# The end of an RG-LRU mixer: gating of the last head by halves on two engines, last products by halves, weight splitting and router scaling on GpSimd

## The chip, the core and the metric

The kernel runs on one core of a Trainium2 chip. The metric is the device time of one execution in microseconds. The engines are TensorE (PE, with its weight loads as PEld), VectorE (DVE), ScalarE (ACT), GpSimd (POOL) and SyncE (SP), which issues the weight transfers. Each executes its own instructions in program order, and semaphores order them against each other.

## The reference

A latent stream of 256 tokens of width 1024 runs through two layers, with 256 context tokens as a prefix. Layer 0 has a bidirectional RG-LRU mixer, layer 1 a spatial-gating mixer, and a mixture of 64 experts stands behind each. All is float32. The part that matters here is the output of the first mixer and the router behind it:

```python
for d in range(2):                                   # both directions
    a_x, b_x = lru_coeffs(flip(ux), ...)
    b_x = b_x.at[:, 0].add(a_x[:, 0] * h_c[:, -1])   # start from the context's state
    yx = yx + flip(linear_scan(a_x, b_x))
out_x = (jax.nn.gelu(gate_x) * yx) @ w_out           # width 1280 = 5 heads x 256
...
x = x + g1 * yx
hx = rmsnorm(x, ffn_norm_g[i]) * (1.0 + sc2) + sh2
scores = jax.nn.sigmoid(jnp.dot(hx, router_w))       # top 8 of 64, by groups
```

## The kernel before

Features lie on the partitions: a head of 256 features is two feature tiles, jt = 0 and jt = 1, of 128 partitions x 256 tokens. Float32 products are made from fp32r parts: each operand x is split into hi = fp32r(x) and lo = x - hi, and `mm3` (line 311) issues hi*hi, hi*lo and lo*hi. Weights come from memory as 1 MB tiles of 128x2048 in a ring. `splitter` (line 555) makes their parts: ScalarE casts hi (wh, line 566), and VectorE or GpSimd, as `split_eng` (line 709) says, subtracts lo (wl, line 567). In this mixer a tile is split by two halves of 128x1024, and four buffers hold wh and wl, so two tiles.

The schedule is written by hand: an engine's instructions stand in the order in which the Python program issues them. The list plan0 gives the order of the steps: for each head h a step A (input projection and convolution), C (gate projection, gelu), B (recurrence gates), mixed with steps F (products of the modulation weights), then O(0) to O(3) and Q. O(i) makes the output products of two of the eight output tiles with the features of heads 0 to 3 (48 products of 128x256 each), and Q adds those of head 4 (48 products in all) for all eight. `ready(n)` makes the weight parts up to number n be split. Step O(i) first splits the tile of O(i+1), so O(0) splits the rest of O(1), O(1) the two halves of O(2), O(2) those of O(3), and O(3) those of Q.

The recurrence itself is in `B_end` (line 860), one call for each feature tile: a multiply of 128x1024, four scans of 128x256 and one add on VectorE. The calls for head 4 are issued by `release()` in O(0), behind that step's `ready`, for jt = 0, and in O(1), behind that step's `ready`, for jt = 1. Behind the second one `gated(4)` follows: multiply by the gelu gate in place (line 902), cast to zh (line 909), subtract to zl (line 910), all on VectorE and 128x512, both feature tiles at once.

Ahead of O(2) a `Tail` is made. Its constructor scales the router weights by s2 on VectorE (rws, line 597; s2 itself at line 511), and issues 16 small products on TensorE. In Q, each of four steps adds 12 products to one PSUM bank, `tail.flush()` issues the router's products for the previous two output tiles, and `tail.add` puts the finished output into the residual stream (line 608), squares it on ScalarE (line 617) and adds the squares on GpSimd (line 621). Behind the last flush the MoE starts: the norm, the routing on VectorE, and the order of the experts, which the queue of the expert weights waits for (line 376).

Of the kernel before, what the change touches and what calls it, by code (L numbers as in the profile page):

```python
# [10 lines left out]
F32 = mybir.dt.float32  # L11
# [4 lines left out]
OP = mybir.AluOpType  # L16

P = 128
D = 1024
KD = 8  # L20
T = 256
# [282 lines left out]
def _body(nc, tc, a, pp, rp, ps, ps1, dr):  # L304
    V, S, G, PE = nc.vector, nc.scalar, nc.gpsimd, nc.tensor
    st = Stream(nc)

    def mm(out, lhsT, rhs, start, stop):
        PE.matmul(out, lhsT, rhs, start=start, stop=stop, skip_group_check=True)  # L309

    def mm3(out, wh, wl, xh, xl, start, stop):

        mm(out, wh, xh, start, False)
        mm(out, wh, xl, False, False)
        mm(out, wl, xh, False, stop)
# [194 lines left out]
    def scale_of(out, sc, g):  # L510
        V.scalar_tensor_tensor(out=out, in0=sc, scalar=1.0, in1=g, op0=OP.add, op1=OP.mult)
# [43 lines left out]
    def splitter(tmp, tiles, eng, bufs=4, per=1):  # L555

        out = []

        def get(q, last=None):
            while len(out) < min(q + 3, last or 4 * len(tiles)):  # L560
                i, c = divmod(len(out), 4)
                n = 512 * per
                t = st.tile(tiles[i])[:, 512 * c:512 * c + n]
                hi = tmp.tile([P, n], F32R, name="wh", bufs=bufs)
                lo = tmp.tile([P, n], F32R, name="wl", bufs=bufs)
                S.copy(out=hi, in_=t)  # L566
                eng(i, c).tensor_tensor(out=lo, in0=t, in1=hi.bitcast(F32), op=OP.subtract)  # L567
                out.extend((hi[:, o:o + 512], lo[:, o:o + 512]) for o in range(0, n, 512))
                if c + per == 4:
                    st.free(tiles[i])  # L570
            return out[max(q, 0)]

        return get

    def cut(parts, c):
        return [x[:, c * P:c * P + P] for x in parts]

    class Tail:


        def __init__(self, tmp, l, gain, rw, name, bufs, per=2, some=6):
            self.per, self.some = per, some
            self.tmp, self.l, self.gain, self.router = tmp, l, gain, rw is not None
            self.name, self.bufs = name, bufs

            self.csh = rs_d[:, 1, 0:64]
            self.p = ps1.tile([P, 512], F32, name="s")
            self.ss = self.p[:, 192:194]
            self.rt = self.p[:, 0:128].rearrange("p (t e) -> p t e", t=2)
            self.sh = self.p[:, 128:192]  # L590
            self.first = True
            self.pend = []
            if rw is not None:
                s2 = later["s2"]
                self.rws = rws = tmp.tile([P, 8, 64], F32, name="rws", bufs=1)
                scale_of(s2, mod[:, l, 4, :], later["ffng"][:, l, :])
                V.tensor_tensor(out=rws, in0=rw, in1=s2.unsqueeze(2).to_broadcast([P, 8, 64]), op=OP.mult)
                for k in range(8):
                    self._mm(self.sh, mod[:, l, 3, k:k + 1].to_broadcast([P, P]), rw[:, k, :], k == 7)

# [39 lines left out]
    def mixer0(rx):  # L640
      with tc.tile_pool(name="m0", bufs=1) as mp, tc.tile_pool(name="m0t", bufs=2) as tp:
# [6 lines left out]
        zh = mp.tile([P, 10, T], F32R, name="zh")  # L648
        zl = mp.tile([P, 10, T], F32R, name="zl")
        ys, gs = {}, {}  # L650
        rw = mp.tile([P, 8, 64], F32, name="rw")
# [26 lines left out]
        for half in range(2):  # L678
            q = [qc[k // 4] if half else qx[:, k:k + 4] for k in (0, 4)]
# [3 lines left out]
            q = q[0]  # L683
# [19 lines left out]
        s2 = mp.tile([P, 2, 10], F32, name="s2")  # L703
# [4 lines left out]

        def split_eng(i, c):
            kind, j = plan0[users[i]]  # L710
            return G if (kind, j) == ("A", 0) or kind == "O" else V


        base = 8
        wq = splitter(tp, [2] + [base + i for i in users[1:]], split_eng, 4, 2)

        def ready(n):
# [142 lines left out]
        def B_end(h, jt, y, ta, te, ti):  # L860
            V.memset(te[:, 0, T:T + 1], 0.5)
            V.memset(te[:, 1, 2 * T - 1:2 * T], 0.5)
            V.tensor_tensor(out=ti, in0=ti, in1=te, op=OP.mult)
            for d in range(2):
                r_, s_, i_ = ta[:, d, :], te[:, d, :], ti[:, d, :]
                rv = (lambda z: z[:, ::-1]) if d else (lambda z: z)
                V.tensor_tensor_scan(rv(s_[:, T:]), rv(r_[:, T:]), rv(i_[:, T:]), 0.0, OP.mult, OP.add)
                last = T if d else 2 * T - 1
                dst = s_[:, :T] if d else y[:, jt, :]
                V.tensor_tensor_scan(rv(dst), rv(r_[:, :T]), rv(i_[:, :T]), s_[:, last:last + 1], OP.mult, OP.add)  # L870
                if d:
                    V.tensor_tensor(out=y[:, jt, :], in0=y[:, jt, :], in1=dst, op=OP.add)
            if jt:
                if h < 4:
                    done.append(h)
                else:
                    gated(h)()

        def Cg(i, q):
            p = bank()  # L880
# [10 lines left out]
        ob = {}  # L891

        def release():
            if held:
                if not rooted:
                    roots()
                rooted.popleft()
                B_end(*held.popleft())

        def gated(h):  # L900
            yv, gv = ys.pop(h), gs.pop(h)
            V.tensor_tensor(out=yv, in0=yv, in1=gv, op=OP.mult)

            def parts():
                hi, lo = (z[:, 2 * h:2 * h + 2, :] for z in (zh, zl))
                if h < 3:
                    S.copy(out=hi, in_=yv)
                else:
                    V.tensor_copy(out=hi, in_=yv)
                V.tensor_tensor(out=lo, in0=yv, in1=hi.bitcast(F32), op=OP.subtract)  # L910

            return parts
# [9 lines left out]
                        j == 0 and f == 0, False)  # L922

        def Q(_, q):
            wq(q + 1)
            for i in range(4):
                for j in range(2):
                    for f in range(2):
                        mm3(ob[i][:, j * T:(j + 1) * T], *cut(wq(q + 2 * f + i // 2), 2 * i % 4 + j), zh[:, 8 + f, :], zl[:, 8 + f, :],
                            False, f == 1)  # L930
                tail.flush()
                for j in range(2):
                    tail.add(2 * i + j, ob[i][:, j * T:(j + 1) * T])
# [745 lines left out]
```

## Time and profile before

| | |
|---|---|
| median of 3 runs | 1469.41 us (1467.08 to 1471.1) |
| profiled execution | 1469.6 us |
| its span, first to last instruction | 1467.7 us |
| mean granted TensorE clock | 0.980 |
| TensorE busy | 1392.4 us (95%) |
| VectorE busy | 753.6 us (51%) |
| ScalarE busy | 518.7 us (35%) |
| GpSimd busy | 331.8 us (23%) |
| moved by DMA | 514.85 MB, mean 351 GB/s |

The times of the profile are counted from the first instruction; the first mixer ends at about 248 us. A busy share is an average over stages with different limits, so the stretch of the change has to be read by itself: what each engine did there in order of time, and which wait ended last. A row of a timeline gives the start, the duration, the engine, the line, the operation, the tile written and the tiles read, and in brackets the idle time of the engine ahead of it with what ended it. The granted clock is given as a share of the upper level of 2.4 GHz.

### The profile page before, as it was taken

What the parts mean: (1) busy time and instruction counts of PE and PEld (TensorE: products, weight loads), DVE (VectorE), ACT (ScalarE), POOL (GpSimd) and SP (SyncE); (2) the same over time, 40 slices, a digit from 0 to 9 for tenths busy, and PEclk for the clock granted to TensorE, in tenths of its full rate; (3) what the DMA queues carried; (4) which work ended last, traced back from release to release, by engine and by line L of the source; (5) the groups of instructions that cost most, each with busy time, mean ns of one, the idle gap of its engine ahead of it and who ended that gap; (6) DMA issues with size and microseconds to landing.
All of it is one profiled execution on the core that took longest, in us unless ns stands there. A gap on an engine that the chain in (4) does not pass through costs nothing. (4 is left out here: it accounts for less than half of the span.)

```text
span 1467.7 us, 27203 instructions
## 1 busy us (share of the span) xinstructions
PE 1392.4 (95%) x10752; PEld 973.3 (66%) x10752; DVE 753.6 (51%) x1375; ACT 518.7 (35%) x874; POOL 331.8 (23%) x415
## 2 busy tenths in 40 slices
PE   6999997899999999999999999899999999999997
PEld 4677776656566575666657899775656666566664
DVE  6789997524343333334346786542334334343534
ACT  4777882422122222222225445432212222212222
POOL 1300044421222112312001451431212212111210
PEclk9999999899999999999999999999999999999999
DMA  9876694589989999999999744369999999999994
GB/s 376 321 276 245 245 375 186 222 351 409 412 362 405 420 420 420 420 418 421 420 418 388 289 163 173 116 251 412 394 389 372 421 421 421 420 419 420 420 420 182
DMA packets 77443, 514.85 MB, mean 351 GB/s; under 512 B 9856, under 2 KB 10240, under 8 KB 17024
## 3 DMA queue, kind: packets, MB, share of 16 engines
q1 hardware_dynamic: 74720, 508.91, 85.3%
q10 hardware_dynamic: 2592, 4.16, 0.9%
q8 instruction: 86, 1.41, 0.4%
q14 instruction: 45, 0.37, 0.1%
HBM read 511.99 MB, written 1.05 MB: 350 GB/s over the span
## 5 line engine op out<-in xcount | busy, mean ns | idle before, releaser
L309 PE MATMUL b<-wr,xg 128*32 128x512 f32 (+2 forms) x1464 | 306.5, 600 | 4.6 <-DMA wr<-in_m_gu 2.9
L567 POOL TENSOR_TENSOR wl<-wr,wh 128x512 fp32r<-128x512 f32 (+1 forms) x82 | 121.2, 1492 | 704.5 <-ACT wh L566 654.5
L309 PE MATMUL b<-wx,xg 128*32 128x512 f32 (+2 forms) x744 | 234.3, 598 | 1.7 <-SPq L1430 1.4
L566 ACT CAST wh<-wr 128x512 fp32r<-128x512 f32 (+1 forms) x230 | 147.4, 682 | 84.5 <-PE b L309 44.8
L567 DVE TENSOR_TENSOR wl<-wr,wh 128x512 fp32r<-128x512 f32 (+1 forms) x148 | 145.4, 1010 | 57.6 <-ACT wh L566 57.4
L309 PEld LDWEIGHTS b<-wr,xg 128*32 128x32 f32 (+2 forms) x1464 | 83.9, 118 | 134.9 <-issue 119.5
L1159 DVE SCALAR_TENSOR_TENSOR xT<-b,mod,xT 128x256 f32<-128x256 f32 x304 | 130.0, 478 | 60.5 <-PE b L309 54.5
L309 PE MATMUL s<-hh,wh 128*128 128x256 f32 x512 | 152.3, 297 | 1.1 <-ACT wh L566 1.1
L309 PE MATMUL s<-hh,wl 128*128 128x256 f32 x512 | 145.5, 284 | 3.7 <-DVE wl L567 1.9
L1526 DVE TENSOR_TENSOR h<-h,b 128x256 f32<-128x256 f32 x44 | 18.5, 420 | 252.4 <-ACT h L1525 252.4
L309 PE MATMUL s<-hl,wh 128*128 128x256 f32 x512 | 144.7, 283 | 0.0
L309 PE MATMUL b<-wr,ht 128*32 128x512 f32 (+2 forms) x712 | 141.9, 596 | 1.5 <-ACT ht L1535 1.5
L1549 DVE SCALAR_TENSOR_TENSOR Y<-b,gt,Y 128x512 fp32r<-128x512 f32 x88 | 65.8, 750 | 150.8 <-ACT Y L1548 150.8
L1525 ACT ACTIVATE h<-b 128x256 f32<-128x256 f32 x44 | 16.9, 384 | 351.0 <-PE b L309 351.0
L309 PEld LDWEIGHTS s<-hh,wh 128*128 128x128 f32 x512 | 98.2, 192 | 28.7 <-issue 25.3
L309 PE MATMUL b<-wx,ht 128*32 128x512 f32 (+2 forms) x392 | 109.1, 595 | 0.5 <-ACT ht L1535 0.5
L1548 ACT ACTIVATE Y<-b,gt 128x512 fp32r<-128x512 f32 x88 | 60.3, 687 | 135.8 <-PE b L309 129.5
L309 PEld LDWEIGHTS s<-hh,wl 128*128 128x128 f32 x512 | 98.1, 192 | 4.8 <-DVE wl L567 2.5
L1407 POOL TENSOR_SCALAR S<-cst,agq 128x32 fp32r<-128x32 f32 (+3 forms) x208 | 83.2, 429 | 72.2 <-PE b L309 54.5
L567 POOL TENSOR_TENSOR wl<-wx,wh 128x512 fp32r<-128x512 f32 (+1 forms) x36 | 53.6, 1506 | 199.2 <-ACT wh L566 192.6
L309 PEld LDWEIGHTS s<-hl,wh 128*128 128x128 f32 x512 | 98.3, 192 | 0.4
L309 PE MATMUL b<-S,xt 128*128 128x256 f32 x704 | 94.5, 287 | 0.0
(283 smaller groups left out, 2744.3 us busy)
## 6 DMA issues: line engine op xcount, KB each, us to landing
wr<-in_m_gu SPq DMA_DIRECT2D x167, 1024.0 KB, 12.7
wx<-in_m_gu SPq DMA_DIRECT2D x89, 1024.0 KB, 12.8
wr<-in_m_dn SPq DMA_DIRECT2D x80, 1024.0 KB, 11.1
wx<-in_m_dn SPq DMA_DIRECT2D x42, 1024.0 KB, 11.4
wr<-in_ada_w SPq DMA_DIRECT2D x32, 1024.0 KB, 9.1
wr<-in_a_in SPq DMA_DIRECT2D x10, 1024.0 KB, 8.1
wr<-in_ada SPq DMA_DIRECT2D x8, 1024.0 KB, 12.2
wr<-in_b_out SPq DMA_DIRECT2D x6, 1024.0 KB, 7.2
```

The lines of the kernel that those rows point to most:

```text
L309: PE.matmul(out, lhsT, rhs, start=start, stop=stop, skip_group_check=True)
L566: S.copy(out=hi, in_=t)
L567: eng(i, c).tensor_tensor(out=lo, in0=t, in1=hi.bitcast(F32), op=OP.subtract)
L1159: V.scalar_tensor_tensor(out=xT[:, d, :], in0=y, scalar=mod[:, l, 5, d:d + 1], in1=xT[:, d, :], op0=OP.mult, op1=OP.add)
L1407: (G if b else V).tensor_scalar(out=s[:, tt, i * P + o:i * P + o + wd], in0=C["iota1"][:, j:j + wd], scalar1=agq[:, tt, q:q + 1], scalar2= ...
L1525: S.activation(out=h, in_=p[:, :256], func=AF.Silu)
L1526: V.tensor_tensor(out=h, in0=h, in1=p[:, 256:], op=OP.mult)
L1548: S.activation(out=hi, in_=p, func=AF.Copy, scale=gts[g])
L1549: V.scalar_tensor_tensor(out=y[:, 1, 512 * c:512 * c + 512], in0=p, scalar=gts[g], in1=hi.bitcast(F32), op0=OP.mult, op1=OP.subtract)
```

## The change

Four edits at the end of the first mixer:

- The gating of head 4 is done for each feature tile in its own `B_end`: for jt = 0 on GpSimd, for jt = 1 on VectorE, each with a multiply, a copy and a subtract of 128x256. The joint gating on VectorE goes.
- Q is issued in two passes: the products with feature tile 0 (weight parts of the first half of its tile) for all four banks, then those with feature tile 1, with the flush and the additions behind each bank.
- The Q tile's low parts are split by GpSimd, as those of the O tiles are.
- The router weights are scaled by GpSimd.

```diff
-                V.tensor_tensor(out=rws, in0=rw, in1=s2.unsqueeze(2).to_broadcast([P, 8, 64]), op=OP.mult)
+                G.tensor_tensor(out=rws, in0=rw, in1=s2.unsqueeze(2).to_broadcast([P, 8, 64]), op=OP.mult)
...
-            return G if (kind, j) == ("A", 0) or kind == "O" else V
+            return G if (kind, j) == ("A", 0) or kind in "OQ" else V
...
-            if jt:
-                if h < 4:
+            if h < 4:
+                if jt:
                     done.append(h)
-                else:
-                    gated(h)()
+                return
+
+            e = V if jt else G
+            yv = y[:, jt, :]
+            e.tensor_tensor(out=yv, in0=yv, in1=gs[h][:, jt, :], op=OP.mult)
+            hi, lo = zh[:, 8 + jt, :], zl[:, 8 + jt, :]
+            e.tensor_copy(out=hi, in_=yv)
+            e.tensor_tensor(out=lo, in0=yv, in1=hi.bitcast(F32), op=OP.subtract)
...
         def Q(_, q):
+            def part(i, f):
+                for j in range(2):
+                    mm3(ob[i][:, j * T:(j + 1) * T], *cut(wq(q + 2 * f + i // 2), 2 * i % 4 + j), zh[:, 8 + f, :], zl[:, 8 + f, :],
+                        False, f == 1)
+
             wq(q + 1)
             for i in range(4):
-                for j in range(2):
-                    for f in range(2):
-                        mm3(ob[i][:, j * T:(j + 1) * T], *cut(wq(q + 2 * f + i // 2), 2 * i % 4 + j), zh[:, 8 + f, :], zl[:, 8 + f, :],
-                            False, f == 1)
+                part(i, 0)
+            for i in range(4):
+                part(i, 1)
                 tail.flush()
                 for j in range(2):
                     tail.add(2 * i + j, ob[i][:, j * T:(j + 1) * T])
```

## Rows read from the trace of the kernel before

**Rows 1.** Who waited for whom, 196 to 275 us: total, times, longest.
```profile
PE b L309 <- DVE mb L1335: 4.4, 1, 4.4
```

**Rows 2.** Busy time of each engine, granted clock and DMA, 226 to 236 us.
```profile
core 0: us, PE busy (x) PEld busy (x) DVE busy (x) ACT busy (x) POOL busy (x), PEclk, DMA share, GB/s
226.00:236.00 10.00, 4.62 (x28) 3.67 (x26) 9.58 (x17) 0.00 (x0) 0.00 (x0) 0.83 0.30 107
```

**Rows 3.** Timeline of TensorE, 217 to 264 us.
```profile
217.30 0.38 PE L309 MATMUL b<-zh,wl 128*128 128x256 f32 x1 [1.76 <-POOL wl L567]
...
228.41 0.28 PE L309 MATMUL b<-zh,wl 128*128 128x256 f32 x1
232.49 0.41 PE L309 MATMUL b<-zh,wh 128*128 128x256 f32 x1 [3.80 <-DVE zh L909]
...
235.06 0.58 PE L309 MATMUL b<-zh,wl 128*128 128x256 f32 x1 [1.36 <-DVE wl L567]
...
236.19 0.58 PE L309 MATMUL b<-zh,wl 128*128 128x256 f32 x1
236.57 0.41 PE L309 MATMUL b<-zh,wh 128*128 128x256 f32 x1
...
239.13 0.41 PE L309 MATMUL b<-zh,wh 128*128 128x256 f32 x1
...
244.50 0.28 PE L309 MATMUL b<-zh,wl 128*128 128x256 f32 x1
...
259.24 0.56 PE L309 MATMUL s<-hh,wh 128*128 128x256 f32 x1
...
263.56 0.39 PE L309 MATMUL s<-hh,wh 128*128 128x256 f32 x1
```

**Rows 4.** Timeline of VectorE, 213 to 236 us.
```profile
213.70 1.22 DVE L863 TENSOR_TENSOR I<-I,T 128x1024 f32<-128x1024 f32 x1
...
226.05 0.42 DVE L872 TENSOR_TENSOR hf<-hf,T 128x256 f32<-128x256 f32 x1
...
226.53 1.22 DVE L863 TENSOR_TENSOR I<-I,T 128x1024 f32<-128x1024 f32 x1
227.85 0.69 DVE L867 TENSOR_TENSOR_SCAN T<-Tt,I 128x256 f32<-128x256 f32 x1
...
230.73 0.42 DVE L872 TENSOR_TENSOR hf<-hf,T 128x256 f32<-128x256 f32 x1
...
232.99 0.16 DVE L511 SCALAR_TENSOR_TENSOR s<-mod,ffng 128x8 f32<-128x8 f32 x1
233.18 0.69 DVE L597 TENSOR_TENSOR rws<-rw,s 128x512 f32<-128x512 f32 x1
233.79 2.35 DVE L567 TENSOR_TENSOR wl<-wx,wh 128x1024 fp32r<-128x1024 f32 x2
```

**Rows 5.** Timeline of ScalarE, GpSimd and VectorE, 213 to 226 us.
```profile
213.78 1.98 ACT L566 CAST wh<-wx 128x1024 fp32r<-128x1024 f32 x2
214.89 2.35 POOL L567 TENSOR_TENSOR wl<-wx,wh 128x1024 fp32r<-128x1024 f32 x1 [4.30 <-ACT wh L566]
215.03 2.76 DVE L867 TENSOR_TENSOR_SCAN T<-Tt,I 128x256 f32<-128x256 f32 x1
...
217.21 5.52 POOL L567 TENSOR_TENSOR wl<-wx,wh 128x1024 fp32r<-128x1024 f32 x2
...
222.69 2.77 POOL L567 TENSOR_TENSOR wl<-wx,wh 128x1024 fp32r<-128x1024 f32 x1
```

**Rows 6.** Groups by line and shape: busy us, mean ns, idle before.
```profile
L1291 POOL TENSOR_TENSOR Y<-xT,fl 128x256 f32<-128x256 f32 x16 | 11.6, 738 | 0.0
L1407 POOL TENSOR_SCALAR S<-cst,agq 128x32 fp32r<-128x32 f32 x124 | 42.9, 373 | 0.0
L909 DVE CAST zh<-hf 128x512 fp32r<-128x512 f32 x2 | 0.9, 427 | 0.1
```

**Rows 7.** Timeline of GpSimd, 248 to 252 us.
```profile
248.67 2.52 POOL L567 TENSOR_TENSOR wl<-wx,wh 128x512 fp32r<-128x512 f32 x2 [3.54 <-ACT wh L566]
```

**Rows 8.** What the queue of weight loads waited for, 180 to 340 us.
```profile
SPq L376 <- DVE order L1368: 12.0, 1, 12.0
```

## The prediction

> **What bounds the kernel now.** I read three views in this order: the list of who waited for whom between 196 and 275 us, the TensorE timeline of the same stretch, and the timelines of the engines that the waits name. The profiled execution took 1469.6 us: a span of 1467.7 us and 1.9 us around it. The median of the runs is 1469.41 us, so the profile is a typical run, and I count from 1469.6.
>
> TensorE has two large waits there: 3.8 us for the gated output of head 4 at the end of the first mixer [rows 3], and just behind it 4.4 us for the routing mask (tile mb) [rows 1]. The TensorE timeline shows what surrounds the first one. Step O(2) waits for its first low weight part and goes on at 217.30, after 1.76 us of idle time. From there O(2) and O(3) run without a hole to 228.41: 94 products, 0.119 us apart. Then come 3.80 us of idle time until zh of head 4 is there, a short hole for zl, and 1.36 us for the low weight part of step Q. In all about 5.4 us are lost between 228.7 and 235.06 [rows 3]. The granted clock of 226 to 236 us has a mean of 0.83, so part of it was below the upper level of 2.4 GHz; the products stand 0.213 us apart between 236.57 and 239.13, 1.8 times as far as before, which is what the 1.2 GHz level does [rows 2, 3]. What the engine did before the fall was to stand idle for 3.8 us. The last product of Q starts at 244.50 [rows 3].
>
> VectorE shows why head 4 is late. Its first half (feature tile jt = 0) runs from 213.70 to 226.47 and the second, the same instructions, from 226.53 to 231.15: 12.8 us against 4.62 us [rows 4]. The difference lies under GpSimd: while it splits O(2) and O(3), a scan that takes 0.69 us alone takes 2.76 us. The first split takes 2.35 us, the next ones 2.77 us: each scan ends about 0.55 us after a split ends, and the next split pays about 0.4 us for it. So the two engines take turns, one instruction each [rows 4, 5].
>
> What follows is rigid. The routing of the first MoE starts from this tail, TensorE waits 4.4 us for its mask [rows 1], and the queue of weight loads waits 12.0 us for the expert order that it gives [rows 8]. I find no absolute time behind it that would absorb a shift, so I carry a shift of Q's end to the end of the kernel one to one.
>
> **The change, part by part.**
>
> Four things are meant to go away: the joint gating of head 4 on VectorE (multiply, cast, subtract, 128x512), the two splits of the Q tile on VectorE from 233.79 (2.35 us), the scaling of the router weights there, and the need of every Q product for both halves. All 5.4 us of TensorE idle time ahead of and in Q can go if its operands come before TensorE reaches it.
>
> The cost is in GpSimd's queue. In program order, release() in step O(0) calls B_end for jt = 0, so the three new GpSimd instructions stand behind the second split of O(1) and ahead of both splits of O(2). GpSimd executes in order. Their first operand is the sum that VectorE finishes at the end of jt = 0. Queued behind this wait are O2a and O2b (the first and second half tile of O(2)), then the router scaling, O3a, O3b, Qa, Qb; TensorE waits for each. In the profile O2a started at 214.89, as soon as ScalarE's cast of 213.78 was there [rows 5]. It can't any more.
>
> When is y(jt = 0) ready? GpSimd is now idle while VectorE works on it, so I give it the undisturbed length: 213.70 + 4.62 = 218.32 [rows 4]. GpSimd starts at about 218.40. VectorE goes straight on with jt = 1: one 128x1024 multiply (1.22 us), four scans, one add. They collide with GpSimd's new instructions. A 128x256 tensor-tensor takes 0.74 us on GpSimd [rows 6]. A GpSimd copy isn't in the trace: the lower bound is the 128x32 scalar operation at 0.37 us, the upper the two-input 128x256 operation at 0.74 us [rows 6]. I take 0.74, which has the same width. Its write could also be slower than either, which costs the range some tenths. Taking turns, the multiply loses about 0.95 us to VectorE's long one (my estimate: its 1.22 us less a start of 0.27 that is hidden), each later step 0.4 us to a scan [rows 4, 5]:
> - multiply: 218.40 + 0.95 + 0.74 = 220.1
> - copy: + 0.74 + 0.4 = 221.2
> - subtract: + 0.74 + 0.4 = 222.4
> - O2a: + 2.35 + 0.4 = 225.1
> - O2b: + 2.35 + 0.4 = 227.9.
>
> On this lock the Trainium skill (SBUF — State Buffer, section "Who interferes with whom") says that a GpSimd instruction and a VectorE instruction with two SBUF inputs exclude each other for a whole instruction, which speaks against putting gating on GpSimd beside VectorE's scans. The scans of rows 5 agree; for the 256-wide instructions no run here shows it yet, and without it the chain above would end at 222.9. On the copy, the same skill (GPSIMD Engine Reference, section "Elementwise — side-by-side cycle accounting") gives 769 ns for 512 elements in its best loop, so by an estimate 0.38 us for 256, and the sum would be 0.36 us lower.
>
> The rest of the queue: VectorE's last add ends behind O2b at about 228.2, its half of the gating takes 0.43 + at most 0.43 (the 512-wide cast [rows 6], so I take 0.3) + 0.43, and s2 0.16 [rows 4], to 229.5. Then GpSimd scales the router weights, 128x512 in 1.26 us [rows 7], with bounds of 0.69 (VectorE's own time for it [rows 4]) and 1.5 for the broadcast operand; I take 1.26. It ends at 230.8, O3a at 233.2, O3b at 235.5, Qa at 237.9, Qb at 240.2, each 2.35 us.
>
> TensorE: O(2) goes on at 225.15 in place of 217.30: 7.85 us later. From then it has 94 products of O(2) and O(3), 48 of Q and the tail's. After an idle time of 9.6 us I expect the lower clock. The fall behind 3.8 us of idle time lasted from 232.49 to about 239.35, and the next one, with no holes in it, from 259.24 to 263.56 [rows 3]. With 4.3 to 6.9 us at 0.213, 20 to 32 products lose 0.095 us each, 1.9 to 3.0 us; the same loss in Q now is some 20 products, 1.9 us. That nets 0 to +1.1, and I take +0.2, because the new stretch has no holes. At this pace TensorE wants O2b at 230.2 (there at 227.9), O3a at 233.7 (233.2), O3b at 236.5 (235.5), Qa at 239.4 (237.9), Qb at 242.2 (240.2). No further hole, though O3a has only 0.5 us to spare.
>
> In the last loop each step has 6 products (0.7 us) and 8 router products in place of 12 and 8. VectorE's two additions (0.88 us) run beside that, so its order costs nothing; if that cover failed it would be at most 0.2 us per step. The tiles of O(2), O(3) and Q come free 4 to 10 us later, and the sync queue reloads them that much later with weights of the experts that need no routing. Their products stand in program order behind the 16 steps of the shared expert, whose first product ran at 259.24 [rows 3], more than 18 us behind Qb's split; that covers it. Without the cover up to 4 us would be due, for Q's tile.
>
> Sum: +7.85 (O2a later) - 5.4 (holes at Q) - 0.3 (the small hole before 236.19, where the spacing is 0.5 us [rows 3]) + 0.2 (clock) = +2.3 us. Q's last product then starts at about 246.8. Predicted: 1469.6 + 2.3 = 1471.9 us.
>
> **The rivals.** What this kernel's measurement can tell from no change is about 0.3%, 4.4 us: below 1465.0 is faster, above 1473.8 slower.
>
> Rival 1, the short GpSimd instructions aren't held up by VectorE, or the copy is very short: O2a ends at 222.5 to 222.9, 2.2 to 2.6 us earlier. The time is 1469.5. For it: the turns are shown only for 1024-wide splits. Against it: VectorE's instructions there are the same ones.
>
> Rival 2, slower: a second stall at O(3). O3a stands behind the router scaling, and that behind everything VectorE does for jt = 1. It decides when O3a comes after 233.7, that is when VectorE reaches s2 more than 0.5 us later than 229.5. With 2 us more there, TensorE waits 1.5 us and falls to the lower level once more (1.9 us): 1471.9 + 3.4 = 1475.3. For it: VectorE's turn comes only after each split, and the margin is thin. Against it: GpSimd's chain has no other user.
>
> Rival 3, the change does what it says: the gating on GpSimd doesn't hold up O(2). Then 5.4 us and 1.9 us of clock go, to about 1462.5. It needs y(jt = 0) by 213.8, when its first instruction has just begun [rows 4]; or another order in the queue than the one I read.
>
> **How the numbers follow.** Forecast, 1470.3 to 1473.6: 0.52. Rival 1, 1468 to 1470.3: 0.20. Rival 2, 1473.8 to 1476: 0.20. Rival 3: 0.08. Faster takes rival 3, slower rival 2, the rest is within 0.3%. The range takes the forecast, rival 1 and most of rival 2, with 1 us below for a lower clock that is shorter than I took: 1467.3 to 1475.4.
>
> **What would show it.** Right: GpSimd stands idle until about 218.4, then come three short instructions, O2a ends at 225; TensorE idles 9 to 10 us ahead of O(2)'s first low product, at a lower clock after it, and runs from O(3) into Q without the 3.8 us wait; Q's last product starts near 246.8. Wrong: O2a starting at 214.9, or the three instructions taking over 5 us, or TensorE waiting again at O(3), or a shift at Q that the MoE does not keep.

## The result and the profile after the change

The changed kernel took 1476.05 us (median of 9 runs, 1470.97 to 1482.77), the kernel before 1468.58 us (9 runs, 1466.75 to 1471.69). The ratio is 1.0054 with a 95% interval of 1.0035 to 1.0073, which makes it 7.9 us slower, 5.1 to 10.7 (the two medians lie 7.5 us apart). A second measurement (label c0_after, below) gave 1.0033 (1.0011 to 1.0055). The prediction was 1471.9 us with a range up to 1475.4: the median lies 0.65 us above the range, and the kernel is slower by more than the 0.3% within which the forecast had it.

The profiled execution took 1476.22 us. The top of its page:

```profile
span 1474.1 us, 27214 instructions
...
PE 1393.2 (95%) x10752; PEld 971.4 (66%) x10752; DVE 747.3 (51%) x1371; ACT 518.6 (35%) x874; POOL 341.1 (23%) x422
```

No engine's busy time moved by more than 10 us; what moved is who waits. I count from a mark: the start of VectorE's long multiply for the first half of head 4 (line 863), at 213.70 before [rows 4] and at 215.28 after. The instructions ahead of it are the same in all kernels shown here, and over their profiles the mark lies between 213.25 and 216.44 us, in the changed kernel itself between 213.40 and 216.40. So I don't count these 1.6 us to the change; where they arise is told under what is not accounted for.

GpSimd's timeline after the change, where rows 5 had the splits of O(2) and O(3) from 214.89:

```profile
220.00 1.79 POOL L880 TENSOR_TENSOR hf<-hf 128x256 f32<-128x256 f32 x1 [7.82 <-DVE T L862]
221.86 0.67 POOL L882 CAST zh<-hf 128x256 fp32r<-128x256 f32 x1
222.61 1.03 POOL L883 TENSOR_TENSOR zl<-hf,zh 128x256 fp32r<-128x256 f32 x1
223.60 5.43 POOL L567 TENSOR_TENSOR wl<-wx,wh 128x1024 fp32r<-128x1024 f32 x2
230.72 1.04 POOL L597 TENSOR_TENSOR rws<-rw,s 128x512 f32<-128x512 f32 x1 [1.69 <-DVE s L511]
231.72 9.44 POOL L567 TENSOR_TENSOR wl<-wx,wh 128x1024 fp32r<-128x1024 f32 x4
```

GpSimd stands idle for 7.8 us, because the first of its new instructions waits for VectorE's sum, and O(2)'s two splits come behind them. VectorE beside it:

```profile
215.28 1.22 DVE L863 TENSOR_TENSOR I<-I,T 128x1024 f32<-128x1024 f32 x1
...
219.50 0.42 DVE L872 TENSOR_TENSOR hf<-hf,T 128x256 f32<-128x256 f32 x1
...
219.99 1.22 DVE L863 TENSOR_TENSOR I<-I,T 128x1024 f32<-128x1024 f32 x1
221.31 1.02 DVE L867 TENSOR_TENSOR_SCAN T<-Tt,I 128x256 f32<-128x256 f32 x1
...
224.22 2.64 DVE L870 TENSOR_TENSOR_SCAN T<-Tt,T,I 128x256 f32<-128x256 f32 x1
226.90 2.41 DVE L872 TENSOR_TENSOR hf<-hf,T 128x256 f32<-128x256 f32 x1
...
230.48 0.16 DVE L511 SCALAR_TENSOR_TENSOR s<-mod,ffng 128x8 f32<-128x8 f32 x1
```

The first half, now undisturbed, is done 4.64 us behind the mark (12.8 us before). The turns have moved to the second half: its last scan and its add end 0.5 and 0.3 us behind the two splits. TensorE, with the rows that answer to rows 3:

```profile
226.37 0.58 PE L309 MATMUL b<-zh,wl 128*128 128x256 f32 x1 [9.25 <-POOL wl L567]
226.75 0.42 PE L309 MATMUL b<-zh,wh 128*128 128x256 f32 x1
...
231.66 0.42 PE L309 MATMUL b<-zh,wl 128*128 128x256 f32 x1
...
247.59 0.28 PE L309 MATMUL b<-zh,wl 128*128 128x256 f32 x1
...
249.29 0.60 PE L309 MATMUL s<-onesf,hf 128*128 128x1 f32 x4 [0.57 <-POOL hf L621]
...
251.61 7.91 PE L309 MATMUL b<-wr,stat 128*32 128x512 f32 x56
```

The 3.8 us wait for zh and the waits in Q are gone, and in their place stands a wait of 9.25 us at the start of O(2). The list of waits (total, times, longest) says it in one line, and that the wait for the routing mask has shrunk from 4.4 us [rows 1]:

```profile
PE b L309 <- POOL wl L567: 9.6, 2, 9.2
...
PE b L309 <- DVE mb L1345: 2.2, 1, 2.2
```

The last row of TensorE's fence is the second loss. The 56 modulation products behind the norm took 6.21 us before and take 7.91 us here. The wait for the mask shrinks mainly because these products end 1.7 us later behind the norm; the mask itself comes 10.6 us behind the norm in place of 11.1.

### The profile page after: what moved, and what is told of

Read it like the earlier page. It is cut to its first block, busy times and chain, and to the rows that moved or that the text cites. A ratio compares the mean times of both kernels' runs of the same rounds, so it can differ in the third digit from the quotient of the medians.

```text
span 1474.1 us, 27214 instructions
## 1 busy us (share of the span) xinstructions
PE 1393.2 (95%) x10752; PEld 971.4 (66%) x10752; DVE 747.3 (51%) x1371; ACT 518.6 (35%) x874; POOL 341.1 (23%) x422
## 5 line engine op out<-in xcount | busy, mean ns | idle before, releaser
L567 POOL TENSOR_TENSOR wl<-wx,wh 128x512 fp32r<-128x512 f32 (+1 forms) x38 | 57.9, 1539 | 194.8 <-ACT wh L566 188.2
## 6 DMA issues: line engine op xcount, KB each, us to landing
wr<-in_m_gu SPq DMA_DIRECT2D x167, 1024.0 KB, 12.8
wx<-in_m_dn SPq DMA_DIRECT2D x42, 1024.0 KB, 11.4
```

## The experiments

Four distances tell the kernels apart: where O(2) goes on behind the mark; where the norm of the MoE starts behind the mark (line 542, on VectorE); how long the modulation products behind it take; and how far behind the norm GpSimd starts the slot matrices of the first MoE's second batch (called first batch below, at 281.89 before). From that point to the end the profiled pair is alike: 1185.8 us before, 1185.9 after. Over all profiles this rest varies by 9 us, from 1182.6 to 1191.8, and by up to 7.7 us between two executions of one kernel (y2).

| kernel | ratio to before (95%) | O(2) goes on | norm | modulation | first batch |
|---|---|---|---|---|---|
| before | 1 | 3.60 | 34.14 | 6.21 | 34.05 |
| before, b_look1 | | 3.59 | 34.59 | 6.22 | 34.03 |
| changed | 1.0054 (1.0035 to 1.0073) | 11.09 | 36.44 | 7.91 | 36.46 |
| c0_after | 1.0033 (1.0011 to 1.0055) | 11.09 | 36.26 | 7.62 | 36.98 |
| a_look1 | | 11.09 | 36.47 | 9.09 | 37.73 |
| a_look2 | | 11.09 | 36.55 | 6.22 | 34.05 |
| x1_rws_v | 1.0036 (1.0019 to 1.0053) | 11.09 | 36.51 | 6.21 | 34.06 |
| x2_gate_v | 1.0056 (1.0038 to 1.0075) | 3.59 | 38.41 | 6.21 | 34.06 |
| x3_gate_rws_v | 1.0016 (0.9998 to 1.0034) | 3.59 | 33.95 | 6.21 | 34.06 |
| x4_qsplit_g | 1.0035 (1.0013 to 1.0056) | 3.58 | 35.94 | 6.21 | 34.02 |
| x6_one_pass | 1.0020 (1.0001 to 1.0039) | 11.10 | 36.12 | 6.22 | 34.03 |
| x7_halves_only | 1.0015 (0.9994 to 1.0036) | 3.58 | 35.65 | 6.21 | 34.04 |
| y1_after_some4 | 1.0037 (1.0018 to 1.0055) | 11.09 | 37.33 | 7.91 | 37.25 |
| y1_look | | 11.09 | 37.39 | 7.91 | 37.27 |
| b_some4 | | 3.59 | 35.87 | 6.21 | 34.03 |

The versions in which VectorE does the splits have the long multiply elsewhere; they are counted from the addition of the last modulation chunk (line 473, 0.23 us ahead of the mark), where the kernel before has 34.37.

| kernel | ratio to before (95%) | norm behind line 473 | modulation | first batch |
|---|---|---|---|---|
| x5_all_v | 0.9954 (0.9928 to 0.9980) | 29.19 | 7.76 | 37.14 |
| x5_again | 0.9966 (0.9947 to 0.9984) | 29.10 | 7.85 | 37.21 |
| y2_allv_some4 | 0.9991 (0.9970 to 1.0012) | 32.04 | 8.99 | 37.54 |
| y2_look | | 31.85 | 7.59 | 36.94 |

The theory: GpSimd's in-order queue holds up O(2)'s splits behind the gating. The rivals: the router scaling in that queue is the cost, or the halves and short passes themselves, or VectorE's total work.

**The change once more.**

> The changed kernel as it is, once more. Reference points, counted from the start of the long multiply of head 4's first half (line 863): step O(2) went on 3.6 us behind it before and 11.1 us behind it after the change; the norm behind Q started 34.1 us behind it before and 36.4 us after. Theory (the queue of GpSimd holds up O(2), and a shift at Q's end is carried on): the same 11.1 and 36.4 again. What is open is the 2.5 us that were lost between the norm and the first MoE's first batch, with a lower clock during the modulation products. If the short passes of Q bring that about, it is there again and the ratio is about 1.004 to 1.006; if it was chance, it is gone and the ratio is about 1.002.

All of it came again: 11.09, 36.26, and 2.9 us lost behind the norm. The ratio, 1.0033, is a little under the 1.004 to 1.006 that was expected for this case.

**Router scaling back on VectorE.**

```diff
-                G.tensor_tensor(out=rws, in0=rw, ...)
+                V.tensor_tensor(out=rws, in0=rw, ...)
```

> The change with the scaling of the router weights back on VectorE. Theory (gating in front of O(2)'s splits is the cause): within 1 us of the changed kernel, O(2) still goes on 11 us behind the mark, because O(3)'s splits have some slack. Rival (the scaling on GpSimd, which waits for all that VectorE does for head 4 and stands in front of O(3)'s splits, is the cost): 3 to 5 us faster than the changed kernel.

O(2) goes on at 11.09 and the norm starts at 36.51: the scaling costs nothing where it stands, and this rival falls for the changed kernel. The profile of x1 lost nothing behind the norm, though TensorE's instructions are the same; more on that below.

**Gating of the first half back on VectorE, scaling left on GpSimd.**

```diff
-            e = V if jt else G
+            e = V
```

> The change with the gating of the first half back on VectorE (still by halves); the router scaling stays on GpSimd. Theory of the queue: O(2) goes on 3.6 us behind the mark as before the change, but now O(3)'s splits stand behind the router scaling, which waits for VectorE's last gating, about 15.7 us behind the mark; O(3) starts about 19.5 us behind it, the norm about 38.7: some 2 us slower than the changed kernel, 4 to 5 us slower than before. Rival (only the gating on GpSimd costs): back to the time before or faster.

O(2) is back at 3.59, so it is the gating in GpSimd's queue that delays it. But now O(3) waits. The first row is of TensorE, the second of GpSimd:

```profile
232.62 0.58 PE L309 MATMUL b<-zh,wl 128*128 128x256 f32 x1 [8.54 <-POOL wl L567]
...
229.23 1.04 POOL L597 TENSOR_TENSOR rws<-rw,s 128x512 f32<-128x512 f32 x1 [9.73 <-DVE s L511]
```

GpSimd stands 9.7 us at the router scaling, and O(3)'s splits behind it. The norm comes at 38.41 (38.7 was expected). Either of the two moves alone is enough to block this queue (x1 has the gating alone, x2 the scaling alone), and undoing the gating alone makes it worse.

**Both back on VectorE.** The edits of x1 and x2 together.

> The change with both, gating of the first half and router scaling, back on VectorE; what is left is Q in two passes, gating by halves, and the Q tile split on GpSimd. Theory of the queue, with turns between VectorE and GpSimd: no wait in O(2) and O(3) beyond those before the change; Q's two splits on GpSimd hold up VectorE's second half by some 4 us, the norm starts about 32.9 us behind the mark, 1.3 us earlier than before: ratio about 0.999. Rival (the short passes themselves cost 2 us or more, by waits or by the clock): ratio 1.002 or more.

The norm is at 33.95, 0.2 us better than before and 1 us worse than expected. Two rows of VectorE and two of TensorE show why:

```profile
228.76 2.44 DVE L872 TENSOR_TENSOR hf<-hf,T 128x256 f32<-128x256 f32 x1
231.23 2.48 DVE L880 TENSOR_TENSOR hf<-hf 128x256 f32<-128x256 f32 x1
...
234.19 0.36 PE L309 MATMUL b<-zh,wh 128*128 128x256 f32 x1 [1.25 <-DVE zh L882]
...
240.13 0.36 PE L309 MATMUL b<-zh,wh 128*128 128x256 f32 x1 [2.59 <-DVE zh L882]
```

The add and the first multiply of the gating take 2.4 us in place of 0.4, each under one of GpSimd's splits of the Q tile. TensorE then waits 1.25 us for the first half and 2.59 us for the second. The ratio, 1.0016 (0.9998 to 1.0034), just leaves out the theory's 0.999 and doesn't exclude the rival's 1.002; in the profile the norm shows no cost of 2 us, and nothing is lost behind it.

**Only the split of the Q tile on GpSimd.**

```diff
-            return G if (kind, j) == ("A", 0) or kind == "O" else V
+            return G if (kind, j) == ("A", 0) or kind in "OQ" else V
```

> The kernel before with one part of the change: the Q tile split by GpSimd. The first split of it can start when O(3)'s second ends, under head 4's second half on VectorE. Theory of turns: each of the two splits holds up one VectorE instruction by about 2 us, the gated output comes 4 us later than before, and the 1.7 us that TensorE waited for Q's low weights go: the norm starts about 36.5 us behind the long multiply of the first half (before: 34.1), 2.4 us slower. Rival (VectorE relieved of the two splits, 2.35 us, no collision): the norm at 32 to 32.5, 1.7 us or more faster.

The norm is 1.8 us later than before (2.4 expected), the ratio 1.0035. VectorE was relieved of 2.35 us of work and lost more than that to the turns: two rows of VectorE, one of TensorE.

```profile
226.03 2.44 DVE L872 TENSOR_TENSOR hf<-hf,T 128x256 f32<-128x256 f32 x1
...
228.52 3.27 DVE L863 TENSOR_TENSOR I<-I,T 128x1024 f32<-128x1024 f32 x1
...
236.53 0.55 PE L309 MATMUL b<-zh,wh 128*128 128x256 f32 x1 [6.32 <-DVE zh L909]
```

The wait for zh grows from 3.80 [rows 3] to 6.32 us. The rival, a relieved VectorE, falls. The norm accounts for 1.8 us of the 5.1 us that the ratio gives; the rest isn't traced.

**The change with Q in one pass.** Only `Q` is as before the change.

```diff
-                part(i, 0)
-            for i in range(4):
-                part(i, 1)
+                for j in range(2):
+                    for f in range(2):
+                        mm3(ob[i][:, j * T:(j + 1) * T], ...)
```

> The changed kernel with Q's products in one pass, as before the change. Theory: O(2) still goes on 11.1 us behind the mark, and the norm starts 36.2 us behind it, within 0.5 us of the changed kernel: the order of Q's products costs and gains nothing where O(2) is late. The 0.6 us wait of TensorE for GpSimd's sums of squares ahead of the norm goes. If that wait brings the lower clock in the modulation products behind it, they take 6.2 us here and not 7.6 to 7.9. Rival (the two passes are what costs): the norm at 34 to 35.

As expected: 36.12, so the order of Q's products neither gains nor costs at the norm where O(2) is late. Behind the norm nothing is lost.

**Halves and two passes alone,** with everything on the engines of before: the edits of x3, and the split of the Q tile back on VectorE.

```diff
-            return G if (kind, j) == ("A", 0) or kind in "OQ" else V
+            return G if (kind, j) == ("A", 0) or kind == "O" else V
```

> The kernel before with gating by halves and Q in two passes, and everything on the engines of before (VectorE gates, scales and splits the Q tile). Theory: O(2) goes on 3.6 us behind the mark; TensorE's wait at the end of O(3) ends when VectorE has split the Q tile, which it does behind the second half's gating, so almost nothing is gained: the norm at 34.5 to 35.6 (before 34.1). Rival (halves give TensorE work in the 3.8 us hole): 31 to 32.

The norm is at 35.65, at the end of what was expected: the 3.8 us hole becomes one of 5.43 us, because TensorE now waits for the Q tile's split, which VectorE does last.

```profile
237.02 0.58 PE L309 MATMUL b<-zh,wl 128*128 128x256 f32 x1 [5.43 <-DVE wl L567]
```

**VectorE does all of it.** The edits of x3, and:

```diff
-            return G if (kind, j) == ("A", 0) or kind in "OQ" else V
+            return G if (kind, j) == ("A", 0) or kind == "O" and j < 2 else V
...
-            if i < 2:
+            if i in (1, 3):
                 release()
```

> A version meant to be faster than both: gating by halves and Q in two passes as in the change, but VectorE does all of it (gating, router scaling, and the splits of the tiles of O(2), O(3) and Q), GpSimd only the splits of O(0) and O(1); the first half's recurrence is issued behind O(2)'s splits, the second half's behind Q's. Theory: with GpSimd out of the way a 128x1024 split holds VectorE for 1.22 us in place of the 2.35 us that a GpSimd split holds it up. O(2) goes on at once, O(3) waits 2 to 3 us, the second half's output comes as TensorE finishes Q's first pass; the norm starts about 28.4 us behind the addition of the last modulation chunk (before: 34.4), some 6 us faster, ratio about 0.996. Rival (the end is bound by VectorE's total work, whoever does the splits): within 1 us of before.

> The version in which VectorE does the splits, once more, for a firmer ratio and a second profile. Theory: the norm 29.2 us behind the addition of the last modulation chunk (before: 34.4), 5 us earlier; up to 3 us of that are lost again behind the norm where the lower clock comes. Ratio 0.995 to 0.998.

This version beats both kernels: 0.9954 and 0.9966, with intervals below 1. The norm starts 5.2 us earlier than before, although VectorE has four more splits to do, so its total work doesn't bound this stretch. GpSimd has no instruction between 213.1 and 238.6 us, and VectorE's run at their undisturbed lengths: two splits in 2.36 us, four in 4.62 us. One long wait of TensorE is left ahead of the norm, 2.67 us at O(3). The version changes two things, who splits and when the recurrence is issued, and no run takes them apart.

```profile
216.07 2.36 DVE L567 TENSOR_TENSOR wl<-wx,wh 128x1024 fp32r<-128x1024 f32 x2
...
225.11 4.62 DVE L567 TENSOR_TENSOR wl<-wx,wh 128x1024 fp32r<-128x1024 f32 x4
...
226.38 0.38 PE L309 MATMUL b<-zh,wl 128*128 128x256 f32 x1 [2.67 <-DVE wl L567]
```

Both profiles lose 3.1 to 3.2 us of the gain behind the norm, as the changed kernel does. That leaves some 2 us, where the ratios give 6.8 and 5.0; both profiled executions were slower than the median of their runs, and the difference isn't traced.

**What is lost behind the norm.** Busy times by engine, granted clock, DMA share and GB/s in stretches of 2 us, of the changed kernel and then of x1, whose norm starts at 251.64 as the changed kernel's does at 251.72:

```profile
core 0: us, PE busy (x) PEld busy (x) DVE busy (x) ACT busy (x) POOL busy (x), PEclk, DMA share, GB/s
...
252.00:254.00 2.00, 2.00 (x16) 0.52 (x12) 0.92 (x3) 1.98 (x4) 1.46 (x2) 0.63 0.53 66
254.00:256.00 2.00, 2.00 (x16) 0.55 (x12) 1.85 (x6) 0.71 (x3) 1.05 (x1) 0.52 0.63 266
256.00:258.00 2.00, 2.00 (x24) 0.56 (x20) 1.93 (x20) 1.22 (x3) 1.22 (x1) 1.00 1.07 451
```

```profile
252.00:254.00 2.00, 2.00 (x24) 0.64 (x20) 0.92 (x2) 1.98 (x4) 1.54 (x2) 1.00 0.24 49
254.00:256.00 2.00, 2.00 (x24) 0.65 (x20) 1.85 (x6) 0.70 (x3) 0.98 (x1) 1.00 0.77 315
256.00:258.00 2.00, 2.00 (x22) 0.59 (x11) 1.93 (x19) 1.16 (x3) 1.29 (x2) 1.00 1.05 438
```

For 3.4 us the changed kernel's TensorE was granted about half of 2.4 GHz and made 16 products in 2 us in place of 24. The norm's broadcast stands behind these products, the first instruction of GpSimd's long chain (normalised rows) waits for it, and at the end of that chain a GpSimd split falls into VectorE's building of the slot matrices, which in the kernel before it just missed. In the changed kernel, the first row of VectorE, the others of GpSimd:

```profile
274.57 2.68 DVE L1417 TENSOR_SCALAR S<-cst,agq 128x128 fp32r<-128x128 f32 x10
...
260.65 1.40 POOL L1301 TENSOR_TENSOR Y<-xT,fl 128x256 f32<-128x256 f32 x2 [1.36 <-ACT fl L1297]
...
275.50 1.28 POOL L567 TENSOR_TENSOR wl<-wr,wh 128x512 fp32r<-128x512 f32 x1 [2.06 <-issue]
...
288.18 3.84 POOL L1417 TENSOR_SCALAR S<-cst,agq 128x64 fp32r<-128x64 f32 x10 [11.41 <-ACT xg L1483]
```

And in the kernel before, where the building ends at 270.94 and the split starts at 271.08:

```profile
247.73 6.21 PE L309 MATMUL b<-wr,stat 128*32 128x512 f32 x56
...
255.38 1.45 POOL L1291 TENSOR_TENSOR Y<-xT,fl 128x256 f32<-128x256 f32 x2
...
269.30 1.64 DVE L1407 TENSOR_SCALAR S<-cst,agq 128x128 fp32r<-128x128 f32 x10
...
271.08 2.03 POOL L567 TENSOR_TENSOR wl<-wr,wh 128x512 fp32r<-128x512 f32 x1 [2.92 <-issue]
```

The chain starts 8.9 us behind the norm in place of 7.5, which is 1.4 us, and the building takes 2.68 us in place of 1.64, which is 1.0 us: together the 2.4 us. The tables bear it out: wherever the modulation products take 6.2 us, the first batch comes 34.0 to 34.1 us behind the norm, and wherever they take 7.6 us or more, it comes 36.5 to 37.7 us behind it.

What TensorE did ahead of the fall: two short groups of six 256-column products (0.7 us each) between groups of eight 64-column products, then one-column products behind a wait of 0.57 us for GpSimd's sums of squares. I first held that wait responsible, and took it away by summing fewer tiles on GpSimd, which adds 16 one-column products. The edit stands in the changed kernel for y1, in the version with all on VectorE for y2.

```diff
-                tail = Tail(tp, 0, mod[:, 0, 2, :], rw, "hf", 4)
+                tail = Tail(tp, 0, mod[:, 0, 2, :], rw, "hf", 4, some=4)
```

> The changed kernel with fewer sums of squares on GpSimd in the first mixer's tail (the first four output tiles are summed there and not the first six; TensorE reduces the other four, some 16 more one-column products). Question: why two of three profiles with the two-pass Q and a late O(2) lost 2.4 to 2.9 us between the norm and the first batch of the MoE. There TensorE was at its lower clock during the modulation products, behind a 0.6 us wait for GpSimd's sums. Theory (the wait and the low work around it bring the lower clock): the wait is gone, the modulation products take 6.2 us, the first batch comes 34.0 us behind the norm; the norm itself 36.2 to 36.5 us behind the mark; ratio about 1.0015. Rival (the lower clock comes by chance of the execution, or from something before): 7.6 to 7.9 us and 36.5 to 37.1 us in part of the looks, as in three of the seven two-pass profiles so far.

> A second profile of the changed kernel with fewer sums on GpSimd: 6.2 us for the modulation products again by the theory; by the rival it may be 7.6 to 7.9.

> The version in which VectorE does the splits, with the same smaller number of sums on GpSimd. The version's own profile lost 3.1 us behind the norm by the lower clock. Theory: 6.2 us for the modulation products, the first batch 34.0 us behind the norm, the norm 29 us behind the addition of the last modulation chunk; ratio 0.994 to 0.996. Rival: as for the changed kernel, the loss is there in part of the looks, and the ratio stays at 0.9954.

> A second profile of the VectorE version with fewer sums on GpSimd: 6.2 us for the modulation products again by the theory; by the rival it may be 7.6 to 7.9.

That theory fell. The long wait ahead of the norm did not go, it moved to the first sums; and the lower clock came in all four profiles, with 7.59 to 8.99 us for the modulation products. The wait was no good suspect from the start: it stands, 0.58 to 0.59 us long, also in x1, x7 and a_look2, where the clock stayed up. In y1:

```profile
247.78 0.61 PE L309 MATMUL s<-onesf,hf 128*128 128x1 f32 x4 [0.56 <-POOL hf L621]
...
252.60 7.91 PE L309 MATMUL b<-wr,stat 128*32 128x512 f32 x56
```

The edit also brought the norm later, by 0.9 us in y1 and by 2.8 us in y2 against x5. More one-column products, then, make it no better. To tell the two passes from the small products and from chance, the pair itself was profiled again, unchanged, and the kernel before with the same edit as y1 (b_some4).

> The kernel before, once more, for its profile. The profiles with Q in one pass show no lower clock in the modulation products behind the norm (three of three, 6.2 us), those in two passes do in three of seven, those in two passes with more one-column products in four of four. If the share of small products (64 and 1 columns) ahead of the norm brings the lower clock, it is 6.2 us again, and the first batch comes 34.0 us behind the norm. If it is chance: 7.6 us or more in part of the looks.

> The kernel before (Q in one pass) with the smaller number of sums on GpSimd and so 16 more one-column products on TensorE. If it is the share of small products, and not the two passes as such, the lower clock can appear here too: 7.6 to 7.9 us. If two passes are needed: 6.2 us. The norm some 1 us later than before, 35.1 us behind the mark.

> The changed kernel, once more, for its profile. By the share of small products the lower clock is there in some or all looks (two of two so far): 7.6 to 7.9 us; the norm at 36.3 to 36.5 us behind the mark.

> The changed kernel, once more, for its profile; as for the look before it.

The counts: with Q in one pass the lower clock behind the norm is in none of five profiles (before, b_look1, x4, x6, b_some4), small products or not. With two passes it is in three of four of the changed kernel, both of x5, all four of y1 and y2, and none of x1, x2, x3 and x7: nine of fourteen. If both had the same chance, 0 of 5 against 9 of 14 would come up about once in 46. That points to the two passes and doesn't prove them: a lower clock at 54 us, where the instructions of all kernels are the same, has the same count, none of the five and nine of the fourteen (not the same nine; see what is not accounted for). The timed runs point the same way and are as little proof: with O(2) late, one pass has 1.0020, two passes have 1.0033 to 1.0054, and the intervals overlap. What decides among executions of the same two-pass program (a_look1 against a_look2, with O(2), norm and wait alike) stays open.

## Why the prediction was wrong

**What bounds the kernel, and the queue.** Right. GpSimd's order was the one that I read, y(jt = 0) was ready 4.64 us behind the mark (4.62 predicted), and O2a ended 11.0 us behind it (11.4), O2b 13.8 (14.2), the router scaling 16.5 (17.1), Qb 25.9 (26.5). x2 and x3 show that the gating in the queue causes it.

**The prices on GpSimd.** Multiply 1.79 us with its turn (1.69 predicted), copy 0.67 (1.14 with a turn), subtract 1.03 (1.14), each split 2.71 (2.75). The turns were right for the first multiply and the splits; the copy was the one that was priced too high, by 0.47 us. The estimate from the Trainium skill's GPSIMD Engine Reference (section "Elementwise — side-by-side cycle accounting"), 0.38 us, or 0.78 us with the same turn, was nearer; whether the copy took a turn, the trace doesn't tell. With the exclusion that the Trainium skill states (SBUF — State Buffer, section "Who interferes with whom") the traces now agree for the 256-wide instructions too: the multiply took 1.79 us where such an instruction takes 0.74 [rows 6], and a scan beside them 1.02 us where it takes 0.69 alone.

**TensorE up to the norm.** The sum was right, and partly by luck. Q's last product starts 32.31 us behind the mark; it was 30.80 before: 1.5 us later, where I had summed 2.3; 0.36 us of the difference are O(2), which went on 7.49 us later and not 7.85. From there to the norm it takes 4.13 us in place of 3.34: I had costed the short steps of the last loop at nothing. In them GpSimd's five sums of squares follow each other without a hole, and TensorE waits 0.57 us for them, a wait that stands in no row of before. The two errors of 0.8 us cancel: the norm is 2.30 us later, 2.1 to 2.4 in the four profiles of the changed kernel, each against the first profile of before (1.7 to 2.0 against the second, whose norm is 0.45 us later). The lower clock behind the long wait took 26 products, inside the 20 to 32; over the four profiles it took 17 to 27. At O(3) no hole came in two of them, and one of 0.2 to 0.3 us in c0_after and a_look1.

**The step that failed: "What follows is rigid".** The prediction carried the shift at Q's end one to one to the end. Behind the norm another 2.4, 2.9 and 3.7 us were lost in three of four profiles, and nothing in the fourth, a mean of 2.25 us. With it the norm's shift of 2.3 us becomes 4.5 us, 0.3%, which agrees with the second measurement and lies a little under the first interval (5.1 to 10.7). That these microseconds are lost there is shown; what brings the lower clock in one execution and not in the next stays open. I had looked for something that would absorb a shift and not for something that would add to it: a chain from TensorE's modulation products through the norm's broadcast to GpSimd has no slack there, and its length depends on TensorE's clock. The granted clock of that stretch in before was 1.00, and I did not ask what the new pattern of products ahead of it would do.

**What is not accounted for.** The profiled pair differs by 6.6 us: 1.6 ahead of the mark, 2.3 up to the norm, 2.4 behind it, 0.3 in the rest. The 1.6 us arise at 54 us, where TensorE's granted clock fell to 0.5 for 3.4 us in the changed kernel and not in the kernel before. Two rows of after, then the same two of before:

```profile
54.00:56.00 2.00, 1.02 (x2) 0.83 (x3) 2.00 (x3) 0.60 (x2) 1.92 (x2) 0.64 0.42 172
56.00:58.00 2.00, 2.00 (x6) 1.61 (x5) 1.20 (x2) 0.00 (x0) 1.83 (x5) 0.51 0.40 70
```

```profile
54.00:56.00 2.00, 1.08 (x5) 0.90 (x6) 2.00 (x3) 1.87 (x3) 1.92 (x2) 1.00 0.42 172
56.00:58.00 2.00, 2.00 (x10) 1.65 (x9) 1.14 (x1) 0.00 (x0) 1.83 (x5) 1.00 0.47 94
```

Every profile's mark follows from it: 213.3 to 213.7 us without this fall (a_look2 and both of before among them), 215.1 to 215.4 with 3.4 us of it, 216.2 to 216.4 with 6.8 us (c0_after, a_look1); where VectorE does the splits, line 473 shows the same. All four profiles of the changed kernel together are 7.6 us longer in the mean than the two of before: 1.8 us ahead of the mark, 2.1 up to the norm, 2.3 behind it and 1.5 in the rest, which varies by 9 us over all profiles. So the profiles hold the measured 7.9 us, but the change is shown to cause only the part up to the norm; the part behind it is traced with its trigger open, and whether the other two belong to the change or to the choice of executions, no run here shows.

**The rivals.** Rival 2 had the right sign by another mechanism: its second stall, at O(3) behind the router scaling, came in the changed kernel with 0.3 us at most, so the margin of 0.5 us was nearly used up; it came in x2 with 8.54 us. Rival 1 fell: multiply and subtract took their turns and only the copy was short, so O2a ended 11.0 us behind the mark, where rival 1 had 8.8 to 9.2. Rival 3, whose terms give 1462.3 rather than 1462.5, would have needed another order in the queue.

## What to carry to other kernels

Before moving a step to an idle engine that works in order, list what stands behind it in that engine's queue and when its own operand comes: here three short instructions, 3.5 us in all, made a wait of 1.76 us into one of 9.25, since the splits that TensorE needed next stood behind them. Where GpSimd and VectorE take turns, work given to GpSimd is not free for VectorE: a 128x1024 split on GpSimd made one VectorE instruction 2.0 to 2.1 us longer (an add 2.44 us in place of 0.42, a multiply 3.27 in place of 1.22), and costs VectorE about 1.2 us if it does the split itself. This fits the norm, which came 5.2 us earlier without GpSimd (in x5, with another order too) and 1.8 us later with one more tile on it (x4). And a shift is to be followed past the stage in which it arises, to the first chain without slack.

## What was not expected of the hardware

TensorE's granted clock fell to its lower level in a stretch in which the engine had no idle time longer than 0.57 us: it had short groups of 256-column products between groups of 64-column and one-column products, and it counted as busy 1.43 to 2.00 us in each 2 us of it. The Trainium skill (TensorE: Matmul & The Clock Gate, section "What's actually happening") ties the lower level to how busy the engine has been and gives it as that of an idle engine; here the busy time of the profile did not tell it, and the same instructions kept the upper level in other executions (a_look2, x1). And a GpSimd multiply of 128x512 whose second operand is one column broadcast took 1.04 us, less than the 1.26 us of a split with two full operands of that size [rows 7].
